# Shared projections of k, q and gate with channels as rows and tokens as columns; reciprocal roots and softmax denominators through DRAM

## The chip, the cores and the metric

One core of a Trainium2 chip runs the whole kernel. The metric is the device time of one execution in microseconds, lower is better. TensorE is called PE in the profile (PEld is its weight load), VectorE DVE, ScalarE ACT, GpSimd POOL and the queue that issues the transfers SP.

## What is computed

The reference is a decoder trunk of two layers over 2048 tokens of width 1024, with 8 heads of 128 channels. The first layer is a gated delta rule; the second is an attention with a forget gate whose keys and values are shared. The change lies in the second layer:

```python
def shared_kv(h, kv_norm, kv_w, kv_forget_bias, kv_k_norm):
    u = rms_norm(h, kv_norm)
    k, v, f = jnp.split(u @ kv_w, [FOX_WIDTH, 2 * FOX_WIDTH], axis=-1)
    k = rms_norm(k.reshape(B, L, FOX_HEADS, HEAD_DIM), kv_k_norm)      # per head, over 128 channels
    ...
def fox_mixer(h, k, v, c, w_in, q_norm, w_out):
    q, z = jnp.split(h @ w_in, [FOX_WIDTH], axis=-1)
    q = rms_norm(q.reshape(B, L, FOX_HEADS, HEAD_DIM), q_norm)
    o = fox_attention(q, k, v, c)             # softmax of q.k plus decay, causal
    o = o * jax.nn.silu(z.reshape(B, L, FOX_HEADS, HEAD_DIM))
    return o.reshape(B, L, FOX_WIDTH) @ w_out
```

All is float32. Products of matrices are made of three matmuls of rounded halves (`mm3`: high by high, high by low, low by high).

## The kernel before

The first layer fills the span up to about 1170 us, its output product up to about 1390 us. Then come the shared projections (the first matmul of k starts at 1398.3 us), the attention (2172.6 us, its first transpose of weights) and the last product (2716.0 us to the end).

**Projections** (class `Shared`). The 2048 tokens are handled in two halves. `hprep` has put the normalized hidden state into `hh` and `hl`, 128 channels by 512 tokens for each of 8 channel blocks. `run` (line 828) loops over 16 pieces `i`: four of k, four of q, four of v, four of z, each 256 columns of the weight, which are two heads. `wsplit` (line 806) loads such a piece in two transfers and splits it into `wh` and `wl` on ScalarE and VectorE; pieces alternate between two pools. Inside a piece, four tiles `tp` of 256 tokens follow one another. `project` (line 839) makes one tile: for each of two blocks of 128 tokens and each of 8 channel blocks three matmuls, the tokens' block as weights and 256 weight columns moving, so 48 matmuls into a PSUM tile `pp` of [token, channel]. `finish` (line 853) is written out after the next tile's `project`, so that TensorE has that to do meanwhile. For k and q it squares and sums over a head on ScalarE (line 859), takes the reciprocal root on GpSimd (`rsqrt`, line 118), scales on VectorE (line 865), turns the four blocks with TensorE (line 871) into [channel, token], and after every second tile scales by the gain on ScalarE (line 876) and stores 512 tokens of both heads (line 878). For z it makes tanh on ScalarE (line 891) and one operation on VectorE (line 892) and stores [token, channel] (line 894). The piece `FORGET` of v also holds the 8 columns of the forget gate.

**Attention** (class `Attention`). 8 heads by 4 groups of 512 queries. `scores` is a generator that runs 22 steps ahead: for each of four blocks of 128 queries of a group it makes the scores, their maxima and the exponential with its row sums `ls`. `weights` (line 1126) turns the exponentials with TensorE (line 1134) and splits them, three steps ahead of the product with the values, which is the main loop (line 1176), one step for each block of 128 keys. `gate_load` (line 1141) fetches the group's z, 512 pieces of 512 bytes to a partition block; `gate` (line 1145), at step `j == 2` of the group, takes the reciprocal of the row sums, scales z by it and by a half in four operations (line 1153), turns it with TensorE (line 1155) into a PSUM tile of the scores' pool and copies it to `gT` (line 1157). After the group's last step `ot = po * gT` (line 1204) is stored.

All transfers of these stages are issued by SP, in one order. The list of each engine's instructions is fixed when the kernel is built, by a scheduler that takes the instruction written first among those that its own model holds ready; so an instruction may stand ahead of one that is written before it.

Of the kernel before, what the change touches and what calls it, by code (L numbers as in the profile page):

```python
# [759 lines left out]
class Shared:  # L760
# [67 lines left out]
    def run(self, half, first):  # L828
        k, q2 = self.k, self.q2
        nc = k.nc  # L830
        last = None
        if half == 0:
            self.t = self.q1.tile([P, L // P, H], F32, name="ft")
        for i in range(16):
# [18 lines left out]
            def finish(tp, pp, kind=kind, cp_=cp_, pts=pts, i=i):  # L853
                n = f"{kind}{cp_}_{tp}"
                if kind in "kq":
                    ss = q2.tile([P, 4], F32, tag="kss", name="kss" + n)
                    for i in range(4):
                        junk = q2.tile([P, P], BF16, tag="junk2", name=f"j{n}_{i}")
                        nc.scalar.activation(junk, pp[:, i // 2, i % 2], AF.Square, accum_out=ss[:, i:i + 1])
                    nc.vector.tensor_scalar(out=ss, in0=ss, scalar1=1.0 / P, scalar2=EPS, op0=ALU.mult, op1=ALU.add)  # L860
                    rs = q2.tile([P, 4], F32, tag="krs", name="krs" + n)
                    rsqrt(k, rs, ss, 4)
                    kn = q2.tile([P, 4, P], F32, tag="vt", name="kn" + n)
                    for i in range(4):
                        nc.vector.tensor_scalar(out=kn[:, i], in0=pp[:, i // 2, i % 2], scalar1=rs[:, i:i + 1],
                                                scalar2=None, op0=ALU.mult)
                    if tp % 2 == 0:
                        pts[0] = [self.pr.tile([P, 512], F32, tag=f"tr{i}", name=f"ptr{n}_{i}") for i in range(2)]
                    for i in range(4):
                        o = (tp % 2 * 2 + i // 2) * P  # L870
                        nc.tensor.transpose(out=pts[0][i % 2][:, o:o + P], in_=kn[:, i], identity=k.ident)
                    if tp % 2 == 1:
                        for i in range(2):
                            kt_ = q2.tile([P, 512], F32, tag="kt", name=f"kt{n}_{i}")
                            gain = k.cols[:, C_KN:C_KN + 1] if kind == "k" else k.qns
                            nc.scalar.activation(kt_, pts[0][i], AF.Copy, scale=gain)
                            dst = self.kT if kind == "k" else self.qT
                            nc.sync.dma_start(dst[cp_ * 2 + i, :, (tp - 1) * 256:(tp + 1) * 256], kt_)
# [432 lines left out]
```

## Time and profile before

| | us |
|---|---|
| median of 3 runs | 2905.1 (2903.18 to 2905.47) |
| the profiled execution | 2906.06, of which the span is 2904.3 |
| shared projections, from the first matmul of k | 1398.3 to about 2171 |
| attention, from its first transpose | 2172.6 to 2716.0 |

The profile comes from one execution. Its page gives the chain of work that ended last, which is followed back from the last instruction, and groups of instructions with their mean duration. The trace behind it answers for a stretch of time: how long each engine was busy, and the instructions in order of time. A matmul's duration in the trace overlaps that of the next, so the pace of TensorE is read from the starts. "x4" behind a line of the timeline means that four equal instructions are merged into it; its second number is then from the first one's start to the last one's end. Some matmul records can be missing from a trace, a few in a hundred.

### The profile page before, as it was taken

To read this page: it belongs to the slowest core of one execution; us is meant where nothing else is said; L and a number is where in the kernel's file an instruction comes from. 1 tells how busy PE (TensorE), PEld (TensorE's weight loads), DVE (VectorE), ACT (ScalarE), POOL (GpSimd) and SP (SyncE) were. 2 spreads that over 40 slices of the span, in tenths; PEclk is the share of its full clock that TensorE was granted. 3 is DMA by queue.
4 is the path that set the end of the run, shared out by engine and by line. 5 is a ranking of instruction groups with operands and counts; after the bars stand their busy time and mean duration, and the time that the engine had idled before them with its cause. 6 is when DMAs were issued, how large, how long until landed. Compare 5 with 4: busy or idle time off the path is not lost.

```text
span 2904.3 us, 50700 instructions
## 1 busy us (share of the span) xinstructions
PE 2797.7 (96%) x18406; PEld 2434.2 (84%) x18406; DVE 1715.9 (59%) x5060; ACT 1335.7 (46%) x3695; POOL 704.6 (24%) x712
## 2 busy tenths in 40 slices
PE   7889999999999999899999999999999999999998
PEld 6677788878887788787999999999998888888787
DVE  6776777777777777635333124332329888888422
ACT  5445544454444444434344223443227677676421
POOL 6544211121111111122211000110004444443322
PEclk9999999999999999999999999999999999999999
DMA  7656444444443443636322323223323323332443
GB/s 234 215 163 191 148 153 137 159 151 130 151 158 118 154 137 108 190 116 200 95 88 88 96 95 113 95 88 94 112 82 101 98 91 98 93 96 76 158 140 109
DMA packets 295505, 371.64 MB, mean 128 GB/s; under 512 B 68443, under 2 KB 216150, under 8 KB 294230
## 3 DMA queue, kind: packets, MB, share of 16 engines
q1 hardware_dynamic: 295088, 368.33, 40.0%
q8 instruction: 145, 2.38, 0.4%
q14 instruction: 106, 0.87, 0.1%
q10 hardware_dynamic: 166, 0.06, 0.0%
HBM read 263.40 MB, written 104.92 MB: 127 GB/s over the span
## 4 chain that ended last, share of the span: by engine, by line
PE 66%; DVE 17%; ACT 3%; issue 3%; POOL 2%; DMA 1%; DVEq 0%; POOLq 0%; SPq 0%; ACTq 0%
DVE acc_q L392 4%; PE pt L1134 4%; PE ppv L130 2%; PE ps L132 2%; PE ppq L130 2%; PE ppv L131 2%; PE ppv L132 2%; PE ppq L131 2%; PE ppq L132 2%; PE ppwf L130 2%; PE ppwf L131 2%; PE ppwf L132 2%; PE ppz L130 2%; PE ppz L131 2%; PE ppz L132 2%
## 5 line engine op out<-in xcount | busy, mean ns | idle before, releaser
L130 PE MATMUL pp_q<-xh_q,wh_q 128*128 128x512 f32 x768 | 325.4, 424 | 1.5 <-ACT acc_q L390 0.8
L132 PE MATMUL pp_q<-xh_q,wl_q 128*128 128x512 f32 x768 | 307.2, 400 | 0.0
L131 PE MATMUL pp_q<-xl_q,wh_q 128*128 128x512 f32 x768 | 305.4, 398 | 0.0
L392 DVE SCALAR_TENSOR_TENSOR acc_q<-cx_q,cols,acc_q 128x512 f32<-128x512 f32 x288 | 227.1, 789 | 13.0 <-ACT acc_q L390 9.7
L125 DVE TENSOR_TENSOR pl<-pt,ph 128x512 fp32r<-128x512 f32 (+1 forms) x320 | 191.8, 605 | 37.9 <-ACT ph L124 36.0
L124 ACT CAST ph<-pt 128x512 fp32r<-128x512 f32 (+1 forms) x320 | 161.8, 519 | 90.5 <-PE pt L1134 89.7
L395 ACT ACTIVATE th_q<-acc_q 128x512 f32<-128x512 f32 x96 | 60.6, 632 | 277.1 <-DVE acc_q L392 273.7
L1120 ACT ACTIVATE s<-s,nm 128x128 f32<-128x128 f32 (+15 forms) x128 | 154.3, 1206 | 67.2 <-DVE nm L1118 67.0
L1134 PE MATMUL pt<-ident,s 128*128 128x128 f32 x1088 | 172.1, 273 | 3.3 <-DVE pl L125 2.4
L132 PEld LDWEIGHTS pp_q<-xh_q,wl_q 128*128 128x128 f32 x768 | 145.5, 189 | 33.9
L130 PEld LDWEIGHTS pp_q<-xh_q,wh_q 128*128 128x128 f32 x768 | 146.1, 190 | 27.4 <-ACT acc_q L390 1.3
L131 PEld LDWEIGHTS pp_q<-xl_q,wh_q 128*128 128x128 f32 x768 | 146.0, 190 | 26.4 <-DVE xl_q L240 0.8
L1134 PEld LDWEIGHTS pt<-ident,s 128*128 128x128 f32 x1088 | 133.5, 140 | 33.4 <-DVE pl L125 3.6
L130 PE MATMUL ppk<-wh_k,hh 128*128 128x256 f32 x512 | 147.7, 288 | 2.6 <-issue 2.6
L130 PE MATMUL ppq<-wh_q,hh 128*128 128x256 f32 x512 | 146.8, 287 | 0.0
L130 PE MATMUL ppv<-wh_v,hh 128*128 128x256 f32 (+1 forms) x512 | 144.9, 283 | 0.0
L131 PE MATMUL ppk<-wl_k,hh 128*128 128x256 f32 x512 | 144.6, 282 | 0.0
L132 PE MATMUL ppk<-wh_k,hl 128*128 128x256 f32 x512 | 144.4, 282 | 0.0
L130 PE MATMUL ppz<-wh_z,hh 128*128 128x256 f32 x512 | 144.3, 282 | 0.0
L132 PE MATMUL ppv<-wh_v,hl 128*128 128x256 f32 (+1 forms) x512 | 143.9, 281 | 0.0
L131 PE MATMUL ppv<-wl_v,hh 128*128 128x256 f32 (+1 forms) x512 | 143.9, 281 | 0.0
L132 PE MATMUL ppq<-wh_q,hl 128*128 128x256 f32 x512 | 143.7, 281 | 0.0
(482 smaller groups left out, 8568.2 us busy)
## 6 DMA issues: line engine op xcount, KB each, us to landing
wh_q<-w_d SPq DMA_DIRECT2D x72, 512.0 KB, 3.6
wl_q<-w_d SPq DMA_DIRECT2D x72, 512.0 KB, 4.9
w_d<-wh_q SPq DMA_DIRECT2D x24, 512.0 KB, 4.8
w_d<-wl_q SPq DMA_DIRECT2D x24, 512.0 KB, 3.1
wh_q_z<-w_d SPq DMA_DIRECT2D x24, 512.0 KB, 3.4
wl_q_z<-w_d SPq DMA_DIRECT2D x24, 512.0 KB, 4.3
wr_q<-in_gdn_w_in_dram SPq DMA_DIRECT2D x22, 512.0 KB, 5.7
x_q<-in_x_dram SPq DMA_DIRECT2D x16, 512.0 KB, 4.8
```

The lines of the kernel that those rows point to most:

```text
L124: i = k.nc.scalar.copy(hi, src)
L125: (eng or k.nc.vector).tensor_tensor(out=lo, in0=src, in1=f(hi), op=ALU.subtract)
L130: nc.tensor.matmul(out, ah, bh, start=start, stop=False)
L131: nc.tensor.matmul(out, ah, bl, start=False, stop=False)
L132: nc.tensor.matmul(out, al, bh, start=False, stop=stop)
L392: nc.vector.scalar_tensor_tensor(out=acc, in0=cx[:, j:j + TB], scalar=cw[j], in1=acc, op0=ALU.mult, op1=ALU.add)
L395: nc.scalar.activation(th, acc, AF.Tanh, scale=0.5)
L1120: e = nc.scalar.activation(s[:, 0:w], s[:, 0:w], AF.Exp, bias=nm, accum_out=ls[:, ii:ii + 1])
L1134: nc.tensor.transpose(out=pt[:, ii * P:(ii + 1) * P], in_=Ps[ii][:, j * P:(j + 1) * P], identity=k.ident)
```

## The change

Projections of k, q and z: `project` takes 128 channels of the weight as weights of TensorE and 512 tokens moving, 24 matmuls to a tile; a tile `tp` is now one head (`tp % 2`) of 512 tokens (`tp // 2`), already as [channel, token]. v stays as it was.

`finish` of k and q: ScalarE squares the tile and copies it scaled by the gain (`kn`); TensorE sums the squares over channels, four products with a column of ones; root and reciprocal as before, four numbers to a partition; these go to DRAM as one row of 512, are fetched again into all 128 partitions (`row`, one tile later) and multiplied on VectorE, and the result is stored (`end`, another tile later). `finish` of z stores [channel, token].

Attention: `den_store` takes the reciprocal of the row sums and writes it to DRAM as a row, at the second query block of the next group's scores; `den_load` fetches it into all partitions at step `j == 4 * g` of the group before; `gate` is one operation on VectorE. The transposes of the gate, its PSUM tile and the copy are gone.

```diff
@@ class Shared, run @@
+        rows, ends = [], []
...
+                if kind != "v":
+                    pp = self.pm.tile([P, 512], F32, tag="mm", name="pp" + n)
+                    c = slice(tp % 2 * P, tp % 2 * P + P)
+                    for kt in range(KT):
+                        mm3(nc, pp, wh[:, kt, c], wl[:, kt, c], hh[:, kt], hl[:, kt], kt == 0, kt == KT - 1)
+                    return pp
...
                 if kind in "kq":
+                    sq = q2.tile([P, 512], F32, tag="th", bufs=4, name="sq" + n)
+                    nc.scalar.activation(sq, pp, AF.Square)
+                    kn = q2.tile([P, 512], F32, tag="vt", bufs=5, name="kn" + n)
+                    nc.scalar.activation(kn, pp, AF.Copy, scale=k.cols[:, C_KN:C_KN + 1] if kind == "k" else k.qns)
+                    pss = self.pr.tile([P, 4], F32, tag="tr0", name="pss" + n)
+                    for c in range(4):
+                        nc.tensor.matmul(pss[:, c:c + 1], sq[:, c * P:(c + 1) * P], k.ones[:, 0:1], start=True, stop=True)
                     ss = q2.tile([P, 4], F32, tag="kss", name="kss" + n)
-                    for i in range(4):
-                        junk = q2.tile([P, P], BF16, tag="junk2", name=f"j{n}_{i}")
-                        nc.scalar.activation(junk, pp[:, i // 2, i % 2], AF.Square, accum_out=ss[:, i:i + 1])
-                    nc.vector.tensor_scalar(out=ss, in0=ss, scalar1=1.0 / P, scalar2=EPS, op0=ALU.mult, op1=ALU.add)
+                    nc.vector.tensor_scalar(out=ss, in0=pss, scalar1=1.0 / P, scalar2=EPS, op0=ALU.mult, op1=ALU.add)
                     rs = q2.tile([P, 4], F32, tag="krs", name="krs" + n)
                     rsqrt(k, rs, ss, 4)
...
+                    d = k.dp.tile([512], F32, name="rr" + n)
+                    nc.sync.dma_start(d.rearrange("(c p) -> p c", p=P), rs)
+                    def row(n=n, kn=kn, d=d, dst=(self.kT if kind == "k" else self.qT)[
+                            cp_ * 2 + tp % 2, :, tp // 2 * 512:tp // 2 * 512 + 512]):
+                        rb = q2.tile([P, 512], F32, tag="th", bufs=4, name="rb" + n)
+                        nc.sync.dma_start(rb, d.rearrange("(a n) -> a n", a=1).to_broadcast([P, 512]))
+                        def end():
+                            nc.vector.tensor_tensor(out=kn, in0=kn, in1=rb, op=ALU.mult)
+                            nc.sync.dma_start(dst, kn)
+                        return end
+                    rows.append(row)
+                elif kind == "z":
...
+                    nc.sync.dma_start(self.z[cp_ * 2 + tp % 2, :, tp // 2 * 512:tp // 2 * 512 + 512], vt)
...
             for tp in range(half * 4, half * 4 + 4):
                 pp = project(tp)
+                if ends:
+                    ends.pop(0)()
+                if rows:
+                    ends.append(rows.pop(0)())
                 if last is not None:
                     last[0](*last[1:])
@@ class Attention, run @@
+                    if ii == 1 and i > 0:
+                        den_store(*order[i - 1])
...
         def gate_load(h, g):
-            nc.sync.dma_start(zr, z_d[g * 512:g * 512 + 512, h * P:(h + 1) * P].rearrange("(t p) c -> p t c", p=P))
+            nc.sync.dma_start(zr, z_d[h, :, g * 512:g * 512 + 512])
+        def den_store(h, g):
+            rl = p2.tile([P, 4], F32, tag="rl", name=f"rl{h}_{g}")
+            nc.vector.reciprocal(rl, groups[h, g][1])
+            d = dens[h, g] = k.dp.tile([512], F32, name=f"den{h}_{g}")
+            nc.sync.dma_start(d.rearrange("(c p) -> p c", p=P), rl)
+        def den_load(h, g):
+            d = dens.pop((h, g))
+            rb = dens[h, g, "b"] = pv.tile([P, 512], F32, tag="rb", name=f"rb{h}_{g}")
+            nc.sync.dma_start(rb, d.rearrange("(a n) -> a n", a=1).to_broadcast([P, 512]))
         def gate(h, g):
             zr = zs.pop((h, g))
...
+            nc.vector.scalar_tensor_tensor(out=zr, in0=zr, scalar=0.5, in1=dens.pop((h, g, "b")),
+                                           op0=ALU.mult, op1=ALU.mult)
+            return zr
...
+            if j == 4 * g and order.index((h, g)) + 1 < len(order):
+                den_load(*order[order.index((h, g)) + 1])
```

## Rows read from the trace of the kernel before

**Rows 1.** Page, the chain that ended last: shares of the span by engine.

```profile
PE 66%; DVE 17%; ACT 3%; issue 3%; POOL 2%; DMA 1%; DVEq 0%; POOLq 0%; SPq 0%; ACTq 0%
```

**Rows 2.** Stretches: from:to, length, busy PE, PEld, DVE, ACT, POOL; granted clock, DMA.

```profile
1500.00:1597.00 97.00, 97.00 (x826) 97.00 (x825) 33.39 (x112) 39.88 (x171) 16.13 (x16) 1.00 0.26 88
...
2185.00:2700.00 515.00, 506.41 (x3023) 433.64 (x3024) 445.39 (x1251) 365.24 (x677) 223.44 (x223) 1.00 0.31 94
2730.00:2880.00 150.00, 150.00 (x646) 121.12 (x645) 41.12 (x70) 32.72 (x71) 43.70 (x42) 1.00 0.42 133
```

**Rows 3.** Timeline of TensorE (start, us, instruction): first matmuls of q and v.

```profile
1499.19 0.36 PE L130 MATMUL ppq<-wh_q,hh 128*128 128x256 f32 x1
...
1597.14 0.36 PE L130 MATMUL ppv<-wh_v,hh 128*128 128x256 f32 x1
```

**Rows 4.** Timeline of TensorE in q, around one burst of transposes.

```profile
1553.81 0.28 PE L132 MATMUL ppq<-wh_q,hl 128*128 128x256 f32 x1
1553.92 0.60 PE L871 MATMUL ptrq<-ident,knq 128*128 128x128 f32 x4
...
1554.48 0.29 PE L131 MATMUL ppq<-wl_q,hh 128*128 128x256 f32 x1
```

**Rows 5.** Timeline of TensorE, z and the last stage: ends of unbroken runs.

```profile
1700.06 0.28 PE L130 MATMUL ppz<-wh_z,hh 128*128 128x256 f32 x1
...
1704.08 0.28 PE L131 MATMUL ppz<-wl_z,hh 128*128 128x256 f32 x1
...
2800.05 0.39 PE L130 MATMUL ppwf<-wa,ohwf 128*128 128x512 f32 x1
...
2803.78 0.39 PE L131 MATMUL ppwf<-wa,ohwf 128*128 128x512 f32 x1
```

**Rows 6.** Timeline of TensorE, first layer: four float32 products between matmuls of 512.

```profile
406.16 0.39 PE L132 MATMUL pp_q<-xh_q,wl_q 128*128 128x512 f32 x1
406.39 0.38 PE L566 MATMUL pa_q0g<-w_q0g,kd_q 128*128 128x128 f32 x2
...
407.51 0.39 PE L131 MATMUL pp_q<-xl_q,wh_q 128*128 128x512 f32 x1
```

**Rows 7.** Timeline of the weight loads, two float32 products with 32 columns moving.

```profile
901.04 0.30 PEld L273 LDWEIGHTS pg_q<-g_q,tri 128*128 128x128 f32 x2
901.26 0.30 PEld L274 LDWEIGHTS pg_q<-g_q,ones 128*128 128x128 f32 x2
```

**Rows 8.** Transposes of 32 rows, L253: durations (min/median/max), and four in the timeline.

```profile
L253 PEld LDWEIGHTS pab_q<-ident,abT_q x16: 132/136/139, 31.2 to 895.5; 32*128 32x128 f32 x16
...
609.62 0.32 PEld L253 LDWEIGHTS pab_q<-ident,abT_q 32*128 32x128 f32 x4 [0.36 <-DVE Ti_q1g L480]
```

**Rows 9.** Timeline of TensorE in the attention, one step with the gate.

```profile
2300.82 0.60 PE L1134 MATMUL pt<-ident,s 128*128 128x128 f32 x4
2301.25 0.60 PE L1155 MATMUL pg<-ident,zr 128*128 128x128 f32 x4
2301.61 0.48 PE L130 MATMUL po<-ph,vh 128*128 128x512 f32 x1
...
2303.28 0.48 PE L130 MATMUL po<-ph,vh 128*128 128x512 f32 x1
```

**Rows 10.** Issues of transfers (count, KB each, median us to landing): the two ends.

```profile
wra<-in_fox_w_out_dram SPq DMA_DIRECT2D x4, 1024.0 KB, 7.1
...
c_d<-cT SPq DMA_DIRECT2D x1, 64.0 KB, 1.5
```

**Rows 11.** Timeline of SP in the attention: an issue.

```profile
2303.66 0.46 SPq L1143 DMA_DIRECT2D zr<-z_d  x1
```

**Rows 12.** Groups of instructions (xcount, busy us, mean ns, idle before): VectorE, both stages.

```profile
L892 DVE SCALAR_TENSOR_TENSOR vtz<-thz,ppz 128x512 f32<-128x512 f32 x32 | 22.0, 687 | 121.4 <-ACT thz L891 121.3
...
L1153 DVE TENSOR_SCALAR zr<-zr,rl 128x128 f32<-128x128 f32 x126 | 41.4, 368 | 0.3
...
L125 DVE TENSOR_TENSOR ql<-qr,qh 128x512 fp32r<-128x512 f32 x8 | 17.7, 2209 | 0.0
```

More of the change, by code (lines that the diff above doesn't have):

```diff
@@ L861, in finish @@
                     rs = q2.tile([P, 4], F32, tag="krs", name="krs" + n)
                     rsqrt(k, rs, ss, 4)
[L863 to L878, printed above, removed]
-                else:
-                    vt = q2.tile([P, 2, 2 * P], F32, tag="vt", name="vt" + n)
-                    if i != FORGET:
-                        ppf = pp.rearrange("p j a b -> p j (a b)")
+                    d = k.dp.tile([512], F32, name="rr" + n)
@@ L886, in finish @@
                             nc.vector.tensor_copy(self.t[:, tp * 2 + j], pp[j][:, 256:256 + H])
-                    elif kind == "v":
-                        nc.scalar.copy(vt, ppf)
-                    else:
-                        th = q2.tile([P, 2, 2 * P], F32, tag="th", name="th" + n)
-                        nc.scalar.activation(th, ppf, AF.Tanh, scale=0.5)
-                        nc.vector.scalar_tensor_tensor(out=vt, in0=th, scalar=1.0, in1=ppf, op0=ALU.add, op1=ALU.mult)
-                    dst = self.v if kind == "v" else self.z
-                    nc.sync.dma_start(dst[tp * 256:tp * 256 + 256, cp_ * 256:cp_ * 256 + 256]
+                    else:
+                        nc.scalar.copy(vt, pp.rearrange("p j a b -> p j (a b)"))
+                    nc.sync.dma_start(self.v[tp * 256:tp * 256 + 256, cp_ * 256:cp_ * 256 + 256]
                                       .rearrange("(j p) c -> p j c", p=P), vt)
@@ L904, in run @@
         last[0](*last[1:])
+        while rows or ends:
+            if ends:
+                ends.pop(0)()
+            if rows:
+                ends.append(rows.pop(0)())
     def gates(self):
@@ L1059, in masked @@
             return cm
-        groups = {}
+        groups, dens = {}, {}
         order = [(h, g) for h in range(H) for g in range(4)]
@@ L1124, in scores @@
                     yield
+            den_store(*order[-1])
+            yield
         def weights(h, g, j):
@@ L1141, in gate_load @@
         def gate_load(h, g):
-            zr = zs[h, g] = pv.tile([P, 4, P], F32, tag="zr", name=f"zr{h}_{g}")
-            nc.sync.dma_start(zr, z_d[g * 512:g * 512 + 512, h * P:(h + 1) * P].rearrange("(t p) c -> p t c", p=P))
+            zr = zs[h, g] = pv.tile([P, 512], F32, tag="zr", name=f"zr{h}_{g}")
+            nc.sync.dma_start(zr, z_d[h, :, g * 512:g * 512 + 512])
[8 more added lines that the diff above has]
+            nc.sync.dma_start(rb, d.rearrange("(a n) -> a n", a=1).to_broadcast([P, 512]))
         def gate(h, g):
-            n = f"{h}_{g}"
             zr = zs.pop((h, g))
-            rl = p2.tile([P, 4], F32, tag="rl", name="rl" + n)
-            nc.vector.reciprocal(rl, groups[h, g][1])
-            pg = pp_s.tile([P, 512], F32, tag="s", name="pg" + n)
-            for ii in range(4):
-                nc.vector.tensor_scalar(out=zr[:, ii], in0=zr[:, ii], scalar1=rl[:, ii:ii + 1], scalar2=0.5,
-                                        op0=ALU.mult, op1=ALU.mult)
-                nc.tensor.transpose(out=pg[:, ii * P:(ii + 1) * P], in_=zr[:, ii], identity=k.ident)
-            gT = pv.tile([P, 512], F32, tag="gT", name="gT" + n)
-            nc.scalar.copy(gT, pg)
-            return gT
+            nc.vector.scalar_tensor_tensor(out=zr, in0=zr, scalar=0.5, in1=dens.pop((h, g, "b")),
+                                           op0=ALU.mult, op1=ALU.mult)
+            return zr
         steps = [(h, g, j) for h in range(H) for g in range(4) for j in range(4 * g + 4)]
```

9 lines of the change are left out of this document (8 added, 1 removed).

## The prediction

> **What bounds the kernel now.** First the chain of work that ended last: TensorE holds 66% of it, VectorE 17% [rows 1]. A share of the whole hides stages, so next the busy times by stretch [rows 2]. The change touches two stages, the shared projections and the attention. In the projections of q TensorE has no idle time at all in 97 us, while ScalarE is busy 39.9 us and VectorE 33.4 us of it; in the attention TensorE is busy 506.4 of 515 us, VectorE 445.4, ScalarE 365.2. The granted clock is 1.00 of full speed, the 2.4 GHz level, in all of these rows. So both stages go as fast as TensorE takes its instructions. A matmul's busy time overlaps the next one's, so it is no price: an instruction's price here is what it adds between the starts of its neighbours, read from the timeline of TensorE. Reading those starts for each kind of instruction is all the sum needs.
>
> **The projections: moving 512 instead of 256.** A tile of work was 48 matmuls with 256 columns moving; it becomes 24 with 512, the same product. From one start to another: 34 matmuls of 256 take 4.02 us, 0.1182 each; 16 of 512 in the last stage take 3.73 us, 0.2331 each [rows 5], and that stage's 150 us hold 646 of them, 0.2322 each [rows 2]. I take 0.1182 and 0.2325. A tile: 48 x 0.1182 = 5.674 us before, 24 x 0.2325 = 5.580 us after; 0.094 us less. With 0.230, the gap ahead of the burst in rows 6, 0.15 us less; with 0.235, as far above, 0.03. So doubling the moving size pays 2% and no more: 256 columns already go at nearly the same pace. z has 4 pairs of heads x 8 tiles = 32 tiles: -3.0 us (-4.9 to -1.1). Its tanh, its one VectorE operation and its store keep their size.
>
> **k and q: transposes out, column sums in.** A k or q tile also had 4 transposes. Between the starts around such a burst lie 0.67 us, of which two matmuls explain 0.236: 0.43 us for the burst [rows 4]. All of q in the first half takes 1597.14 - 1499.19 = 97.95 us for 16 tiles [rows 3], 6.122 us a tile, and 5.674 + 0.43 = 6.10 agrees. q's second half and k count as the same. In place of the transposes the change squares the product on ScalarE and sums over channels with TensorE: for each 128 tokens one matmul with 128x128 squares as weights and a single column of ones moving. Both are plain float32, not the rounded type of the projections. The trace shows what plain float32 costs: every such product runs as two passes, each with a load of the weights of its own. Eight passes (four products of 128 columns) stand between two 512-column matmuls, 407.51 - 406.16 = 1.35 us, of which 2 x 0.2325 are the two matmuls': 0.885 us, 0.111 a pass [rows 6]. Is that the moving side or the weights? Where only 32 columns move, pairs of loads still start 0.22 us apart, 0.110 a pass [rows 7]. A quarter of the columns saves nothing, so the load of the weights sets the pace, and one column should cost as much as 32. New burst: 8 x 0.1106 = 0.885 us.
>
> A k or q tile after: 5.580 + 0.885 = 6.465, against 6.122: +0.343 us. There are 2 x 4 x 8 = 64: **+22.0 us**. The bounds of a pass are 0.061 us, the nearest row with 128 columns of weights and few moving, transposes with 32 rows, whose four loads take 0.32 us where one takes 0.136 [rows 8], so (0.32 - 0.136) / 3 from start to start, and 0.12 us, a tenth above rows 6: a tile 6.07 to 6.54, in all -3.5 to +27 us. I take 0.1106, because rows 6 and 7 are of the same type and full depth, and rows 8 of neither.
>
> What else is edited here lies beside TensorE. ScalarE loses four squares with their sums read back and half of two scaled copies, and gets one square and one scaled copy of 128x512; VectorE loses four scalings and gets one multiply; both stay under half busy [rows 2], and a product has the whole next tile, 6 us, to be evacuated before its PSUM buffer is wanted. If that cover went, each us late would be a us. The reciprocal roots now pass through DRAM: a store of 512 numbers of 4 bytes, then a load of that row into all 128 partitions, a multiply, and the store of the result, all on SP's queue. Per tile the queue has a row store that waits for the roots, a broadcast load that waits for that store to land, and a result store that waits for the multiply; the weight loads of the next pair are queued behind these. They are wanted a whole pair later (four tiles, 24 us), and the result waits in one of five buffers, so only a chain longer than a tile reaches TensorE. An issue costs 0.46 us [rows 11]; landings lie between 1.5 and 7.1 us [rows 10]. No row shows a store of 4-byte pieces. I take 3 us, nearer the low end since 2 KB is little, yet twice it since it comes in many pieces: 3 + 2 x 0.46 = 3.9 us, under the 6.46 us of a tile, so nothing.
>
> **Attention: the gate.** Each of the 32 groups of four query blocks loses 4 transposes on TensorE. Four transposes take 2301.25 - 2300.82 = 0.43 us from start to start [rows 9]; since TensorE is the bound, 32 x 0.43 = **-13.8 us**. Beside it, VectorE loses four scalings of 0.368 us [rows 12] = 1.47 us and gets one two-tensor operation of 128x512 from SBUF, between 0.69 us (the one on z's product) and 2.2 us, as the slowest operation on two tensors in SBUF has it [rows 12]: -0.8 to +0.7 us a group of, on average, ten steps; ScalarE loses a copy; the PSUM buffers of the scores lose a user. What comes in is waiting. The store of the row comes at least one step before its broadcast load and the load six steps before the gate; a step, from one product's first matmul to the next's, is 2303.28 - 2301.61 = 1.67 us [rows 9], so 7 x 1.67 = 11.7 us cover two landings (6 us at 3 each, 14 at 7.1). Beyond that VectorE would wait at the gate with the residues of the weights queued behind it, and those are made three steps ahead of their use, 5 us more. SP's other loads stand behind the waiting broadcast for up to one landing. I take no loss; the bound is that the whole gain goes.
>
> **Sum.** +22.0 - 3.0 - 13.8 = +5.2 us on the profiled execution's 2906.1 us, which is 1.0 us above the median of the runs, 2905.1. On the median: **2910.3 us**, 0.18% more: what the gate gives back, the column sums take. This kernel's measurement can tell about 0.2%, 5.8 us, from no change, so the forecast is "hardly different, rather slower".
>
> **Rivals.**
> 1. The single moving column is cheap. If a pass goes by the columns that move, the bursts fall to the 0.061 us a pass of rows 8: 8 x 0.061 = 0.49, a tile 6.07, 64 x -0.054 = -3.5; total -3.5 - 3.0 - 13.8 = -20.3: 2885 us. For it: rows 8. Against it: rows 7, where 32 columns of the right type gained nothing over 128. The Trainium skill (TensorE: Matmul & The Clock Gate, Back-to-back issue gap) lists a matmul of 1 to 64 columns at some 60 cycles, 25 ns, far less than the 110 ns of rows 7 with 32 columns; by that alone, an estimate, a burst would be 0.2 us and the kernel near 2866 us (64 x -0.34 - 3.0 - 13.8).
> 2. The row through DRAM becomes the bound of k and q (slower). It decides once a row's landing exceeds 6.46 - 0.92 = 5.5 us: then SP, in order, needs longer than TensorE for a tile. At 7.1 us it is 8.0 us a tile, +1.56 x 64 = +100; at 6.2 us +42: 2952 us. For it: 512 pieces of 4 bytes, which no row shows, beside weight loads of 512 KB. Against it: rows 10 are the ends of the list of transfers, and only four kinds in it, all of 512 KB or more, land later than 5.5 us. The Trainium skill (DMA: Bandwidth & Descriptors, Rules for kernel authors) lets a last dimension that isn't contiguous cost one descriptor per element, which speaks for it; no row prices one.
> 3. The attention gives nothing: VectorE, busy 86% there, or the new waits at the gate end last instead. +22.0 - 3.0 = +19.0: 2924 us. For it: VectorE's load and its in-order queue; against it: TensorE's idle time of 8.6 us in 515, so VectorE kept ahead with more work.
> 4. TensorE's idle time in the attention goes too, as the scores get back a PSUM buffer: -8.6 more, 2902 us. Little speaks for it; that idle time ends mostly on VectorE.
>
> **How the numbers follow.** Forecast 0.56, with its own range 2902 to 2918, from the bounds of the 512-column gap and of the pass (0.108 to 0.115); rival 1 0.15, rival 2 0.10, rival 3 0.12, rival 4 0.07. The range 2885 to 2927 takes in all but rival 2 and the far ends. Slower by over 0.2% (above 2910.9): 0.25 of the forecast, 0.10 and 0.12: 0.47. Faster (below 2899.3): rival 1, 0.03 of rival 4, 0.02 of the forecast: 0.20. The same: 0.33.
>
> **What would show it.** In the timeline of TensorE in k or q: starts 0.2325 us apart, and a burst of eight short matmuls that adds 0.885 us; 0.5 or less means rival 1. A q stage of 16 tiles lasting 103.4 us (97.95 before), a z stage shorter by 1.5 us. No row of four transposes from the gate, and an attention shorter by 14 us. Gaps of TensorE in k and q that end on ScalarE or a transfer, and landings of the row stores above 5.5 us, would mean rival 2; idle time of VectorE at the gate that ends on a transfer, rival 3. The forecast is wrong if one column moves faster than the weights load, or if any wait on the rows reaches TensorE.

## The result and the profile after

The changed kernel takes 3649.1 us, median of 4 runs (3644.4 to 3651.4), against 2905.2: 1.256 times as long [1.2545, 1.2582], +744 us where +5 was forecast. The profiled execution has a span of 3649.7 us. Run once more, after the other experiments, it took 3507.3 us (below, e19_again), so those are compared with that. By stages, each from its first matmul to that of the next:

| | before | after |
|---|---|---|
| shared projections (k, q, v, z), two halves | 774.3 | 1322.4 |
| of these q, first half (16 tiles) | 97.9 | 239.2 |
| attention | 543.4 | 738.3 |

First the page's chain that ended last, by engine and by line, against [rows 1]:

```profile
PE 28%; DMA 26%; issue 17%; DVE 15%; POOL 3%; ACT 3%; SPq 0%; DVEq 0%; POOLq 0%; ACTq 0%
DMA rrk<-krsk 7%; DMA den<-rl 6%; DMA rrq<-krsq 5%; DVE acc_q L392 3%; DMA rb<-den 3%; PE ppwf L132 2%; PE ppwf L130 2%; PE ppwf L131 2%; PE pt L1156 1%; DMA zr<-z_d 1%; DMA rbk<-rrk 1%; PE pp_q_z L130 1%; PE ppwg L132 1%; PE ppwg L130 1%; PE ppwg L131 1%
```

TensorE falls from 66% to 28%, transfers rise from 1% to 26%, and the first three lines are the stores of the new rows. In the stretches (from:to, length, busy PE, PEld, DVE, ACT, POOL; granted clock, DMA), the first mostly k and q, the last attention, against [rows 2]:

```profile
1600.00:1700.00 100.00, 45.31 (x175) 36.44 (x174) 11.32 (x29) 11.61 (x24) 6.35 (x6) 0.70 0.26 50
...
2740.00:3400.00 660.00, 507.91 (x2700) 427.10 (x2700) 402.08 (x1082) 324.01 (x602) 214.14 (x214) 0.88 0.33 81
```

No engine is busy half of the time in the first. TensorE, busy for 45 of the 100 us, is also granted 0.70 of its clock there, a mean between its two levels of 1.2 and 2.4 GHz, instead of 1.00 before. Who waits for what (us, times, longest), SyncE and VectorE, in the first half of the projections and then in the attention:

```profile
SPq L882 <- DMA rrq<-krsq: 123.5, 15, 10.8
SPq L882 <- DMA rrk<-krsk: 108.3, 14, 10.9
...
DVE knk L885 <- DMA rbk<-rrk: 157.9, 16, 21.0
...
SPq L1178 <- DMA den<-rl: 220.5, 28, 12.4
...
DVE zr L1183 <- DMA rb<-den: 171.1, 22, 11.6
```

How these waits make the pace of a tile stands in the timeline of SyncE and VectorE (start, us, instruction):

```profile
1605.39 0.39 SPq L877 DMA_DIRECT2D rrk<-krsk  x1
...
1616.25 0.32 SPq L882 DMA_DIRECT2D rbk<-rrk  x1
...
1621.51 0.69 DVE L885 TENSOR_TENSOR knk<-knk,rbk 128x512 f32<-128x512 f32 x1 [12.11 <-DMA rbk<-rrk]
1622.12 0.15 DVE L873 TENSOR_SCALAR kssk<-pssk 128x4 f32<-128x4 f32 x1
...
1623.56 0.37 SPq L877 DMA_DIRECT2D rrk<-krsk  x1
...
1634.23 0.33 SPq L882 DMA_DIRECT2D rbk<-rrk  x1
1634.65 0.39 SPq L877 DMA_DIRECT2D rrk<-krsk  x1
```

The read of a row (L882) can be issued only when its store has landed, 10.9 us after the store's issue; it takes 5.3 us; the multiply has been standing at the head of VectorE's list for 12.1 us, and behind it the sums of the next tile (L873), so the next row is stored only 2.1 us after. Two tiles take 10.86 + 5.26 + 2.05 + 11.09 = 29.3 us, 14.6 a tile. These rows are of k's last tiles, while TensorE is already at q; q's 239.2 us by 16 are 14.95.

### The profile page after: what moved, and what is told of

It reads as the page before. It is cut to its first block, busy times and chain, and to the rows that moved or that the text cites. A ratio compares the mean times of both kernels' runs of the same rounds, so it can differ in the third digit from the quotient of the medians.

```text
span 3649.7 us, 45850 instructions
## 1 busy us (share of the span) xinstructions
PE 2959.3 (81%) x16230; PEld 2450.2 (67%) x16230; DVE 1669.9 (46%) x4772; ACT 1281.4 (35%) x3215; POOL 705.7 (19%) x712
## 4 chain that ended last, share of the span: by engine, by line
PE 28%; DMA 26%; issue 17%; DVE 15%; POOL 3%; ACT 3%; SPq 0%; DVEq 0%; POOLq 0%; ACTq 0%
DMA rrk<-krsk 7%; DMA den<-rl 6%; DMA rrq<-krsq 5%; DVE acc_q L392 3%; DMA rb<-den 3%; PE ppwf L132 2%; PE ppwf L130 2%; PE ppwf L131 2%; PE pt L1156 1%; DMA zr<-z_d 1%; DMA rbk<-rrk 1%; PE pp_q_z L130 1%; PE ppwg L132 1%; PE ppwg L130 1%; PE ppwg L131 1%
## 5 line engine op out<-in xcount | busy, mean ns | idle before, releaser
L1156 PE MATMUL pt<-ident,s 128*128 128x128 f32 x1088 | 191.0, 295 | 115.2 <-DVE pl L125 78.8
L1156 PEld LDWEIGHTS pt<-ident,s 128*128 128x128 f32 x1088 | 145.7, 152 | 154.7 <-DVE pl L125 77.0
L871 PE MATMUL pssq<-ones,sqq 128*128 128x1 f32 x256 | 45.0, 297 | 219.7 <-ACT sqq L866 199.1
L871 PEld LDWEIGHTS pssq<-ones,sqq 128*128 128x128 f32 x256 | 45.2, 259 | 227.5 <-ACT sqq L866 226.1
L871 PE MATMUL pssk<-ones,sqk 128*128 128x1 f32 x256 | 43.3, 290 | 167.4 <-ACT sqk L866 167.4
L885 DVE TENSOR_TENSOR knk<-knk,rbk 128x512 f32<-128x512 f32 x32 | 22.1, 692 | 312.7 <-DMA rbk<-rrk 312.5
L885 DVE TENSOR_TENSOR knq<-knq,rbq 128x512 f32<-128x512 f32 x32 | 22.1, 691 | 312.3 <-DMA rbq<-rrq 312.2
L130 PE MATMUL ps<-kh,qh 128*128 128x512 f32 (+2 forms) x320 | 124.5, 389 | 47.8 <-DVE mx L1131 47.6
L1075 POOL TENSOR_SCALAR_AFFINE_SELECT cm<-cd 128x128 f32<-128x128 f32 (+3 forms) x128 | 63.3, 498 | 514.8 <-DVE mx L1131 326.0
L871 PEld LDWEIGHTS pssk<-ones,sqk 128*128 128x128 f32 x256 | 43.7, 251 | 175.3 <-ACT sqk L866 173.8
```

The costliest lines, as they stand in the source:

```text
L130: nc.tensor.matmul(out, ah, bh, start=start, stop=False)
L871: nc.tensor.matmul(pss[:, c:c + 1], sq[:, c * P:(c + 1) * P], k.ones[:, 0:1], start=True, stop=True)
L885: nc.vector.tensor_tensor(out=kn, in0=kn, in1=rb, op=ALU.mult)
L1075: nc.gpsimd.affine_select(out=cm[:, 0:w], in_=cds[h, g][:, g * 512:g * 512 + w], pattern=[[-1, w]], compare_op=ALU.is_ge, fill=NEG, base=P ...
L1156: nc.tensor.transpose(out=pt[:, ii * P:(ii + 1) * P], in_=Ps[ii][:, j * P:(j + 1) * P], identity=k.ident)
```

## The experiments

The stage columns of this table are read as above, each from one profiled execution; a run without an interval is one execution.

| run | us | ratio to before | projections | attention |
|---|---|---|---|---|
| kernel before | 2905 | | 774.3 | 543.4 |
| changed kernel, e19_again | 3507.3 | 1.2069 [1.2049, 1.2089] | 1225.0 | 691.6 |
| e1_no_rows | 2934.7 | 1.0095 [1.0076, 1.0113] | 793.6 | 552.9 |
| e2_kq_alone | 3362.9 | | 1230.7 | 542.9 |
| e3_att_alone | 3054.3 | | 770.0 | 697.6 |
| e4_16b | 2929.3 | | 801.1 | 543.9 |
| e5_ladder | 3287.2 | | 1152.5 | 546.1 |
| e6_lag | 3511.8 | | 1230.4 | 696.8 |
| e8_norows_zr3 | 2936.7 | 1.0102 [1.0085, 1.0119] | 794.3 | 555.5 |
| e9_att16 | 2931.5 | 1.0090 [1.0075, 1.0105] | 769.5 | 574.8 |
| e11_pieces | 2984.2 | | 851.3 | 550.5 |
| e12_lag_forced | 3365.4 | | 1081.5 | 698.4 |
| e13_16b_late | 2936.9 | 1.0109 [1.0095, 1.0122] | 802.6 | 548.3 |
| e14_att16_late | 2916.0 | 1.0038 [1.0025, 1.0052] | 770.3 | 556.6 |
| e15_no_product | 2911.8 | 1.0024 [1.0015, 1.0034] | 794.2 | 527.0 |
| e16_att16_tied | **2893.5** | **0.9959 [0.9944, 0.9974]** | 769.3 | 533.2 |
| e17_att16_pool | 2895.2 | 0.9960 [0.9947, 0.9974] | 769.5 | 534.6 |
| e18_actq | 3325.0 | | 1043.5 | 693.1 |

### The changed kernel once more

**e19_again.** No edit. It was run last, after the two halves of the change (below) had come to 137 us less together than the whole.

> The changed kernel once more, unaltered. Theory, the list of the whole change makes the 137 us that the two parts alone don't show: 3640 to 3660 us again, landings of a row 8.5 us at the least. Rival, landings of such a store differ from one session to another, and the parts were run in a quicker one: near 3510 us (2905 + 458 + 149), landings from 7.4 us.

The rival holds: 3507.3 us. From the store's issue to the read's, a row of k took 11.1 us in the median of 32 in the first run and 9.7 in this one, at the least 9.4 and 7.5; one of q 11.5 and 9.8. The kernel before did not differ between the two (2905.2 and 2907.8). The first run is the odd one: e6_lag (below), whose SyncE list turned out nearly the same, took 3511.8 us in a third session. What made the first session's stores slower isn't shown. About 600 us of loss need an explanation by the change itself.

### Are the rows all of it?

**e1_no_rows.** Every store and read of a row taken out, a tile of ones in its place; the kernel then leaves out the scaling by root and by denominator.

```diff
-                    nc.sync.dma_start(d.rearrange("(c p) -> p c", p=P), rs)
...
-                        nc.sync.dma_start(rb, d.rearrange("(a n) -> a n", a=1).to_broadcast([P, 512]))
+                        rb = self.one
```

> The changed kernel without the rows through DRAM: the roots and the denominators are still computed, but neither stored nor fetched, and the multiplies take a constant tile of ones (the scaling by root and by denominator is left out). Theory A (the wait for the rows is the whole loss, the rest of my sum holds): 2910 us, a q stage of 103 us, an attention some 14 us shorter than before. Theory B (the products moving one column, or the new shapes themselves, hold TensorE up): it stays above 3300 us. Rival 1 of the prediction, a cheap pass: 2885 us.

Without rows 573 of the 600 us are gone. The projections then hold what was priced: in the timeline of TensorE, the matmuls around a burst of column sums and the first ones of q and of v:

```profile
1557.33 0.39 PE L132 MATMUL ppq<-hh,wl_q 128*128 128x512 f32 x1
1557.56 0.95 PE L873 MATMUL pssq<-ones,sqq 128*128 128x1 f32 x8
1558.37 0.48 PE L130 MATMUL ppq<-hh,wh_q 128*128 128x512 f32 x1
1558.68 0.39 PE L131 MATMUL ppq<-hl,wh_q 128*128 128x512 f32 x1
...
1500.27 0.48 PE L130 MATMUL ppq<-hh,wh_q 128*128 128x512 f32 x1
...
1603.54 0.36 PE L130 MATMUL ppv<-wh_v,hh 128*128 128x256 f32 x1
```

From 1557.33 to 1558.68 are 1.35 us, less two matmuls of 0.2325: 0.885 for the eight passes with one moving column, as in [rows 6] with 128 columns. The q stage is 103.3 us. Attention did not go as forecast: 552.9 us, 9.5 longer than before, though its transposes are gone.

**e2_kq_alone, e3_att_alone.** Each half of the change by itself: k and q changed with gate and attention as before, and the reverse.

> Only k and q changed (projection, column sums, roots as rows through DRAM); z and the attention as before. Theory A: the k and q tiles cost about 15.3 us instead of 6.1, so 2905 + 64 x 9.2 = some 3490 us. If the two parts only hurt together (their transfers in one queue), well under 3300 us.

> Only z and the attention changed (gate as one operation, denominators as rows through DRAM); k and q as before. Theory A: the attention waits about 5.5 us in each of 32 groups, 2905 + 176 - 17 = some 3065 us. If the two parts only hurt together, 2890 us.

+458 and +149 us, 607 together, as the whole in e19_again (+600): the two parts add up, and k and q lose three times as much. e2 stays under its 3490 us, which was worked out from the slower rows of the first run; e3 is 11 us off its 3065.

### What makes the store of a row slow?

**e4_16b.** The four numbers of a partition side by side: 128 pieces of 16 bytes instead of 512 of 4. The numbers land in another order, so they scale other tokens.

```diff
-                    nc.sync.dma_start(d.rearrange("(c p) -> p c", p=P), rs)
+                    nc.sync.dma_start(d.rearrange("(p c) -> p c", p=P), rs)
```

> The changed kernel, each row stored as 128 pieces of 16 bytes instead of 512 pieces of 4 (the numbers land in another order, so the scaling is by other tokens' numbers); the same bytes, waits and broadcast loads. Theory A1 (the store's landing goes by its pieces): it lands in 3 to 4 us instead of 10.8, and the kernel falls below 3100 us. Theory A2 (the broadcast load or the mere round trip through DRAM is slow): within 100 us of 3649.

The same bytes cost 578 us less. Timeline of SyncE, e4, a row's store and its read:

```profile
1516.81 0.32 SPq L877 DMA_DIRECT2D rrq<-krsq  x1
1518.27 0.32 SPq L882 DMA_DIRECT2D rbq<-rrq  x1
```

The read follows 1.5 us after the store; over k's rows it is 2.9 in the median, against 9.7 in e19. What is it in the pieces: their number, their size, or where they go?

**e5_ladder, e11_pieces.** Fewer pieces of 4 bytes, and then other shapes. Both kernels scale only the tokens whose numbers are stored. The rows of denominators go as 128 pieces of 16 bytes in e5 and as 512 of 16 in e11 (the diff leaves that out).

```diff
-                    nc.sync.dma_start(d.rearrange("(c p) -> p c", p=P), rs)
+                    m = 1 if kind == "k" else 2                        # e5
+                    d = d[0:m * P]
+                    nc.sync.dma_start(d.rearrange("(c p) -> p c", p=P), rs[:, 0:m])
...
+                    d = k.dp.tile([2048], F32, name="rr" + n)          # e11
+                    m = 2 if kind == "k" else 1
+                    w = m * P
+                    to = d[0:w].rearrange("(p c) -> p c", p=P) if kind == "k" else d.rearrange("(p c) -> p c", p=P)[:, 0:1]
+                    nc.sync.dma_start(to, rs[:, 0:m])
```

> The row of a key tile is stored as 128 pieces of 4 bytes, that of a query tile as 256 pieces of 4 bytes (only the first 128 and 256 tokens of a tile are scaled, the others are left out), a row of denominators as 128 pieces of 16 bytes. Theory, the landing goes by the number of pieces (10.8 us for 512, 1.4 to 3 for 128 of 16 bytes): near 2.9 us in the key stage, 5.5 us in the query stage, so that the key stage runs near 104 us as with no rows and the query stage between 104 and 130; the whole 2930 to 2960 us. Rival, the size of a piece decides and not the number: landings of 8 us and more in both stages, and over 3200 us.

> Other shapes of the row's store: for k 128 pieces of 8 bytes side by side (256 of a tile's tokens are scaled), for q 128 pieces of 4 bytes each 64 bytes from the next (one token is scaled), for the denominators 512 pieces of 16 bytes, each number four times (the gate's factors are then not those of its tokens). Before, 128 pieces of 4 bytes side by side landed in 7.7 us, 512 in 10.8, 128 of 16 bytes in 1.4. Theory 1, a piece under 16 bytes is slow wherever it goes: landings of 6 to 8 us in k and in q, key and query stages near 170 us, and the denominators' 512 pieces below 5 us with attention near 544 us; the whole about 3250 us. Theory 2, neighbours written into the same place hold each other up: q's spread pieces land in 1.4 to 3 us and its stage goes at 104 us; k's stay above 5 us; the whole about 3120 us. Rival to both, the number alone: the 512 pieces of 16 bytes land in over 8 us and attention takes over 600 us.

A landing is read where SyncE has nothing to do but wait for it, from the store's issue to the issue of the read. Timeline of SyncE, e5: 128 pieces of 4 bytes:

```profile
1523.15 0.32 SPq L879 DMA_DIRECT2D rrk<-krsk  x1
1531.00 0.32 SPq L884 DMA_DIRECT2D rbk<-rrk  x1
```

Timeline of SyncE, e11: 128 pieces of 8 bytes, 128 of 4 bytes each 64 bytes from the next:

```profile
1453.42 0.32 SPq L880 DMA_DIRECT2D rrk<-krsk  x1
1456.39 0.32 SPq L886 DMA_DIRECT2D rbk<-rrk  x1
...
1626.13 0.32 SPq L880 DMA_DIRECT2D rrq<-krsq  x1
1627.60 0.32 SPq L886 DMA_DIRECT2D rbq<-rrq  x1
```

From the store's issue to the read's, over all rows of a stage (the median holds what else SyncE did in between):

| pieces | where | run, rows | least us | median us |
|---|---|---|---|---|
| 512 of 4 bytes | side by side | e19, k | 7.5 | 9.7 |
| 256 of 4 bytes | side by side | e5, q | 7.6 | 9.2 |
| 128 of 4 bytes | side by side | e5, k | 6.8 | 8.0 |
| 128 of 8 bytes | side by side | e11, k | 2.7 | 3.7 |
| 512 of 16 bytes | side by side | e11, denominators | 2.4 | 3.7 |
| 128 of 16 bytes | side by side | e4, k | 1.4 | 2.9 |
| 128 of 4 bytes | 64 bytes apart | e11, q | 1.4 | 1.5 |

The theory of e5, that the number of pieces decides, falls: a quarter of them still takes 8.0 us and the kernel 3287 us. So does the first of e11, that every small piece is slow: 4 bytes alone are quick when the neighbour is 64 bytes away. Its second holds for q, but put k's pieces of 8 bytes above 5 us, and they took 3.7. What is slow is many pieces of 4 bytes side by side. Whether it is the same few bytes that count, or pieces that follow each other in time, was not tried, nor were 512 pieces set apart. A rule of the Trainium skill (DMA: Bandwidth & Descriptors, Specifications) has transfers under 512 bytes read, modify and write. It would fit pieces that hold each other up at one place, but no run shows that step itself, and all pieces of this table are under 512 bytes, the quick ones too.

### Can the landing be hidden?

**e6_lag, e12_lag_forced, e18_actq.** The row read one tile later (e6), the read fixed behind the next row's store (e12), or the stores moved to ScalarE's queue (e18, from e6). All three have more buffers for the tiles that wait (the diff leaves that out).

```diff
-                if rows:
+                if len(rows) > 1 or rows and kind not in "kq":                 # e6, e12, e18
                     ends.append(rows.pop(0)())
...
+                        with k.tc.issue_after(lr[-1]):                         # e12: behind the last row's store
+                            nc.sync.dma_start(rb, ...)
...
-                    nc.sync.dma_start(d.rearrange("(c p) -> p c", p=P), rs)
+                    nc.scalar.dma_start(d.rearrange("(c p) -> p c", p=P), rs)  # e18
```

> Each row is read back one tile later than in the changed kernel, so that two stores of rows are under way at once; attention is left as it is changed. Theory, what costs is the round trip standing in SyncE's list between two stores of rows: two tiles share one landing of 10.8 us, a tile of k or q goes from 15 us to 7.5 to 9 us, and the whole to 3200 to 3270 us. Rival, the store of 512 pieces holds its queue for the 10.8 us: a tile stays at 10.8 us or more, and the whole is 3380 us or more.

> As the run with the row read one tile later, but with the read of a row fixed behind the next row's store in SyncE's list, which the scheduler had put back in the run before; attention is as changed. Theory, the 10.8 us are a landing that several rows can share: SyncE's wait for a row falls from 7 to 11 us to under 5 us, a tile of k or q takes 6.5 to 8 us and the whole 3130 to 3230 us. Rival, one store of 512 pieces of 4 bytes holds its queue for the whole time: a tile stays at 10.8 us or more and the whole near 3510 us.

> As the run with the row read one tile later, with the stores of the rows of k and q issued from ScalarE's queue, all else from SyncE's. Theory, a store of 512 pieces of 4 bytes holds only the queue that it is in: the reads and stores of SyncE's queue go on, a tile of k or q takes 6.5 to 8 us and the whole 3130 to 3230 us. Rival, it holds the engines that move all queues' data: a tile stays at 10 us or more and the whole at 3350 us or more.

e6 did not test its theory: in SyncE's list the scheduler had moved the read back, right behind its own store, and the time is that of e19_again. In e12 the order held and SyncE's waits for the store vanished, yet a q tile took 11.1 us (177.2 by 16, against 214.6 by 16 = 13.4 in e19), and the whole 3365 us, 142 less than e19 and far from the theory's 3130 to 3230. Timeline of SyncE and VectorE, e12:

```profile
1601.02 0.37 SPq L877 DMA_DIRECT2D rrq<-krsq  x1
1601.48 0.46 SPq L883 DMA_DIRECT2D rbq<-rrq  x1
...
1610.42 0.69 DVE L886 TENSOR_TENSOR knq<-knq,rbq 128x512 f32<-128x512 f32 x1 [10.51 <-DMA rbq<-rrq]
```

And the view of that store's tile, for the store of 1601.02 alone:

```profile
DMA to landing us min/median/max: 9.2/9.2/9.2
```

The read is of the row before, which has landed (SyncE issued it without a wait), but it is done only 8.9 us after its issue, 9.4 after the unrelated store ahead of it and 0.2 after that store's landing. In all 17 such pairs of e12 whose store's landing the trace has, the read is back 0.2 to 0.8 us after it. So going on issuing hides little: what is issued behind such a store comes back with it. Is that the queue? Timeline, e18, where the stores are on ScalarE's queue:

```profile
1623.81 0.37 ACTq L877 DMA_DIRECT2D rrq<-krsq  x1
1628.43 0.32 SPq L882 DMA_DIRECT2D rbq<-rrq  x1
1628.84 0.39 SPq L819 DMA_DIRECT2D wr_q<-in_fox_w_in_dram  x1
1634.95 0.69 DVE L885 TENSOR_TENSOR knq<-knq,rbq 128x512 f32<-128x512 f32 x1 [12.27 <-DMA rbq<-rrq]
1636.09 0.38 SPq L882 DMA_DIRECT2D rbq<-rrq  x1
1639.32 0.69 DVE L885 TENSOR_TENSOR knq<-knq,rbq 128x512 f32<-128x512 f32 x1 [3.67 <-DMA rbq<-rrq]
```

With a store under way on the other queue, the read of 1628.43 is back after 6.5 us, 11.1 after that store; with none under way, the next is back after 3.2. (The 13 reads of e18 that stand 4 to 6 us behind a store took 4.8 to 6.8 us, 6.2 in the median.) A load of weights (1628.84) stands behind the first as well, as behind all 13; but 18 reads with such a load and no store under way were back after 4.0 us in the median, at most 5.3. So a store on the other queue holds the read too. The Trainium skill (DMA: Bandwidth & Descriptors, Queues, rings and completion order) says that a transfer's signal lands only after every earlier write of the same transfer engine, across its queues; the trace agrees: of the 13 reads the four behind a store whose landing it has were back 0.2 to 0.6 us after that landing. It shows only when the read is reported done, not when its data came.

The other queue helped little: a tile took 10.6 us, 10 or more as the rival has it, though the whole, 3325 us, lies between theory and rival. The test isn't clean, since the move also lets ScalarE stand at the stores until the roots are ready, up to 17.5 us at a time.

### Why does attention gain nothing?

Once rows were cheap (e4) or absent (e1), attention still took 544 to 553 us where the forecast was 530.

**e8_norows_zr3, e9_att16.** The theory of both: the gate's factors now stay in z's tile until the output's product, so z's next load comes late. e8 adds a third buffer to e1. e9 puts k and q back as before, keeps rows of 16-byte pieces, restores their order by strided views, and writes the gate's product into the row's tile.

```diff
-            zr = zs[h, g] = pv.tile([P, 512], F32, tag="zr", name=f"zr{h}_{g}")
+            zr = zs[h, g] = pv.tile([P, 512], F32, tag="zr", bufs=3, name=f"zr{h}_{g}")    # e8
...
+            rb = dens.pop((h, g, "b")).rearrange("q (p c) -> q c p", p=P)                  # e9
+            nc.vector.scalar_tensor_tensor(out=rb, in0=zr.rearrange("q (c p) -> q c p", p=P), scalar=0.5, in1=rb,
+                                           op0=ALU.mult, op1=ALU.mult)
```

> As the run without any row (the norms' roots and the denominators are replaced by 1), with a third buffer for the gate's tile. Theory, attention's gain was lost because the gate's tile is now held until the output's product, so that the next z is loaded late and VectorE stands: with the third buffer attention falls from 552.9 us to about 530 us (543.4 before, less 13.8) and the whole from 2934.7 to about 2912 us. Rival, the attention stage is set by the matmuls and scores themselves: 548 to 553 us, and 2930 to 2935 us.

> Keys and queries as in the kernel before; gate projected by channel, denominators as rows of 128 pieces of 16 bytes, put in order by the product's view, and the gate's product written into the row's tile, so that z's tile is free at once. Theory, the gate's tile was what attention lost by: attention near 530 us, the whole 2888 to 2893 us, faster than before. Rival, attention gains nothing from the gate without transposes: 543 to 550 us, the whole 2902 to 2910 us.

The theory falls twice: 555.5 and 574.8 us. VectorE's wait for z was the same with a third buffer, and e9 paid for its views: the gate's and the output's product took 1.12 and 1.08 us in the median, 0.69 and 0.68 in e1. Waits of VectorE in e1 and in e8:

```profile
DVE zr L1183 <- DMA zr<-z_d: 42.8, 26, 3.0
```

```profile
DVE zr L1183 <- DMA zr<-z_d: 47.5, 26, 4.0
```

The product stands in VectorE's list close behind the load that it needs, as in the timeline of SyncE and VectorE, e1:

```profile
2350.16 0.43 SPq L1167 DMA_DIRECT2D zr<-z_d  x1
...
2354.06 0.69 DVE L1183 SCALAR_TENSOR_TENSOR zr<-zr,one 128x512 f32<-128x512 f32 x1 [2.27 <-DMA zr<-z_d]
2354.67 0.55 DVE L125 TENSOR_TENSOR pl<-pt,ph 128x384 fp32r<-128x384 f32 x1
```

VectorE comes to the product 1.6 us after the load's issue (2.5 in the median of 32, in e8 too) and stands 2.27 us; the weights' residues (`pl`) are behind it.

**e13_16b_late, e14_att16_late.** The product written at the group's last step, in e4 and in a kernel with k and q as before.

```diff
-            if j == 2:
+            if j == 4 * g + 3:
                 gT = gate(h, g)
```

> As the run with rows of 128 pieces of 16 bytes (numbers land in another order, so they scale other tokens), with one line moved: the gate's product is written at a group's last step instead of its third. Theory, attention's gain was lost because VectorE's product stands ahead of work of the weights and waits for a row or for z that has not landed (28 us in all): attention falls from 543.9 to 530 to 535 us and the whole from 2929 to 2915 to 2920 us. Rival, TensorE's saved transposes only become waits for VectorE's residues of the weights: 540 to 545 us, and 2925 to 2930 us.

> Keys and queries as in the kernel before, gate projected by channel, denominators as rows of 128 pieces of 16 bytes put in order by the view of one operand of the gate's product, which is written at a group's last step. Theory, without the early product attention takes 530 to 535 us and the whole 2887 to 2895 us, faster than before. Rival, the strided operand (the product took 1.50 us with three strided views, 0.69 without) and waits for VectorE eat it: 543 to 550 us of attention, 2900 to 2907 us.

No gain again. But the waits of e13, VectorE's and TensorE's, say why the test missed:

```profile
DVE zr L1183 <- DMA rb<-den: 21.7, 13, 3.1
...
PE pt L1156 <- DVE pl L125: 17.4, 21, 1.4
```

VectorE still stands 21.7 us at the row: the list hardly moved, since the scheduler takes what its model holds ready. In e4 and in e13 alike the product stands 56 instructions of VectorE ahead of the output's product (median of 32 groups). TensorE's wait for the residues was 2.4 us in the kernel before:

```profile
PE pt L1134 <- DVE pl L125: 2.4, 1, 2.4
```

**e15_no_product, e16_att16_tied, e17_att16_pool.** The product taken away (from e1); the product tied behind the group's last residue (from e14); the product on GpSimd, its half folded into the reciprocals (from e14).

```diff
-                gT = gate(h, g)
+                with tc.issue_after(pls[h, g]):          # e16
+                    gT = gate(h, g)
...
-            nc.vector.scalar_tensor_tensor(out=z4, in0=z4, scalar=0.5, ...)
+            nc.gpsimd.tensor_tensor(out=z4, in0=z4, ...)   # e17
```

> As the run without any row, and without the gate's product: the output is multiplied by z as it was loaded (the norms' roots, the half and the denominators are left out). Theory, VectorE's stand at the product (42.8 us in 26 waits, and 22 us of work) is what attention lost by: attention falls from 552.9 us to 530 us or less, the whole from 2934.7 to about 2912 us. Rival, TensorE's saved transposes turn into waits for VectorE's residues whatever the gate does: attention stays at 545 to 553 us, the whole at 2927 to 2935 us.

> As the run with keys and queries as before and the gate's product written late (attention 552.4 us, the whole 2916.0), with the product fixed behind the last residue of the group's weights in VectorE's list. Theory, the 25 us of VectorE's waits for the row and for z go, since both have landed by then: attention 530 to 537 us, the whole 2892 to 2900 us. Rival, the product then stands right ahead of the output's product and the 1.40 us that it takes with its strided operand delays the next group: 545 us or more, the whole 2908 us or more.

> As the same run (attention 552.4 us, the whole 2916.0), with the gate's product on GpSimd, the half folded into the reciprocals. Theory, VectorE loses 44.6 us of work and 25 us of waits: attention 528 to 535 us, the whole 2890 to 2898 us, faster than before. Rival, GpSimd, busy 236 of 552 us, stands at the product in its turn and hands the residues of keys and values on late, or TensorE waits for VectorE all the same: 545 us or more, the whole 2908 us or more.

All three land on the theory. e15's and e16's attention (stretches), and e16's product and TensorE's wait for the residues:

```profile
2194.00:2720.00 526.00, 511.09 (x2991) 433.80 (x2991) 439.76 (x1164) 366.82 (x676) 232.51 (x232) 1.00 0.32 100
```

```profile
2170.00:2692.00 522.00, 507.70 (x2968) 429.57 (x2966) 450.35 (x1181) 359.80 (x672) 236.62 (x229) 1.00 0.39 114
...
L1179 DVE SCALAR_TENSOR_TENSOR zr<-zr,rb 128x512 f32<-128x512 f32 x32 | 37.9, 1184 | 0.0
...
PE pt L1150 <- DVE pl L1155: 2.4, 7, 0.9
```

The product now stands 9 instructions ahead of the output's. It no longer waits (0.0), though it takes 1.09 us in the median with its strided operand, and TensorE's wait for residues is back at 2.4 us. Between e14 and e16 the tie is the only difference: attention goes from 556.6 to 533.2 us. e16 keeps k and q of the kernel before and is 0.4% faster than it; e17 the same, with GpSimd doing the waiting.

## Why the prediction was wrong

**The failed step** is the price of the row's store: "No row shows a store of 4-byte pieces. I take 3 us, nearer the low end since 2 KB is little". The read behind it could go only 10.9 us after its issue. Bytes were the wrong measure; the bounds, 1.5 to 7.1 us from rows of other shapes [rows 10], didn't hold it either, and an unseen shape of transfer deserved a wider range than the rows could give.

**Rival 2** named the place and the point from which it decides (5.5 us), at a chance of 0.10, and its price was low. By its own formula 10.9 us gives 11.8 a tile, +5.4 x 64 = +343 us. The projections lost 548 (451 in e19), for the step left something out: the multiply waits at the head of VectorE's list with the next tile's sums behind it, so the read's 5.3 us and the next root stand in the loop as well, 14.6 us a tile. The sum of 3.9 us held the store alone. "Only a chain longer than a tile reaches TensorE" was right, and the chain was longer than two tiles of 6.46 us.

**Attention, -13.8.** The size was about right, the cover wrong. Without the product attention is 16.4 us shorter than before (e15), with it tied behind the residues 10.2 (e16). But "7 x 1.67 = 11.7 us cover two landings" failed twice. From a row's store to its read alone went 9.7 us in the median. And the steps were counted as written: VectorE came to the product in the median 2.0 us before the row's read was even issued. SyncE waited 220.5 us for the rows of denominators, and VectorE 171.1 at the gate. Even with no row at all the list puts the product so close behind z's load that the stage is 9.5 us longer (e1, where the granted clock was 0.98 besides). The wait is rival 3's mechanism, "the new waits at the gate"; it said 2924 us, e1 has 2934.7.

**What held.** The pace of 512 moving columns and the burst of 0.885 us, so rival 1 is out; a q stage of 103.4 us, measured 103.3; z alone -3.0, measured -4 to -5 in e3, e9, e14, e16 and e17, at the edge of its bounds. That the projections grow by 19.3 us in e1, for +19.0 from k, q and z, is in part luck. q's +10.8 for +11.0 is the forecast's. But k's two stages lasted 100.9 and 106.1 us before, not q's 97.95, and grew by 4.6 instead of 11.0, while a gap of 7.8 us came in that nothing forecast: the transposes of the second half's hidden state, once between k's first matmuls, now stand ahead of them, since a tile needs 512 tokens. With rows and product free the whole takes 2911.8 us (e15); the forecast was 2910.3, but with the product, so that is luck as well. The sum was that of a kernel whose new waits cost nothing.

**Left open:** whether small pieces hold each other up because they share a place or because they follow at once, and why the first session's rows took 1.4 to 1.8 us longer than those of e19.

## What to carry to other kernels

Before passing a small vector through DRAM, look at how its pieces lie: one line that let each partition write its four numbers side by side was worth 578 us here. The numbers then land in another order; views that put it right were run for the gate alone, at 0.4 us a product. An operation that depends on a transfer belongs in an in-order list behind the work that doesn't wait, tied there if a scheduler makes the list: the tie alone turned +13 us of attention (e14) into -10 (e16). And a gain that is priced on the bound engine is only had if the engine that feeds it, here VectorE with the residues, isn't given a wait in exchange.

## What the hardware showed unexpectedly

- From the store's issue to the read's, 128 pieces of 4 bytes took 8.0 us side by side and 1.5 us when 64 bytes apart; 512 of 16 bytes, four times the bytes of the slow row, took 3.7 us (medians).
- A read issued behind a slow store is reported done 0.2 to 0.8 us after that store's landing, on the same queue (17 of 17 pairs) and, issued 4 to 6 us behind it, from another (4 of 4). On the other queue such reads took 6.2 us in the median instead of 4.0.
- The same kernel took 3649 and 3507 us in two sessions, with rows of k answered in 11.1 and 9.7 us, while the kernel without them stayed within 0.1%.
- A product of 128x512 on VectorE took 0.69 us with contiguous operands and 1.08 to 1.12 (medians) with one operand read, or read and written, at steps of 16 bytes.
